# One more seven-product pair in the second FFN of a two-layer decoder trunk: parts of 7, 8 and 7 pairs

## The chip, the cores and the metric

The kernel runs on one core of a Trainium2 chip. The metric is the device time of one execution in microseconds (us). Engines: PE is the matrix engine (TensorE), ACT the scalar engine, DVE the vector engine, POOL is GpSimd, and SP issues most transfers. POOL issues transfers too: those that add into their destination.

## What is computed

Two layers work on 528 positions (16 meta tokens and 512 real ones) of width 1024. Each layer has a mixer and a feed-forward part (FFN), both with a norm before and a norm after:

```python
def ffn_sublayer(h, pre_g, post_g, w_up, conv_w, w_down):
    u = rms_norm(h, pre_g)
    z = jnp.einsum("bld,df->blf", u, w_up)          # 1024 -> 2 x 2816
    z = causal_depthwise_conv(z, conv_w)            # 3 taps
    g, up = jnp.split(z, 2, axis=-1)
    y = jnp.einsum("blf,fd->bld", jax.nn.silu(g) * up, w_down)
    return h + rms_norm(y, post_g)
```

The mixer holds an attention of 8 heads with a forgetting gate, a convolution branch and a short convolution, and ends in a product with `w_out`. Everything is float32.

## The kernel before

**Products.** Each float32 operand is split into a high and a low half (`whi`, `wlo` for a weight, `uhi`, `ulo` for the activations), and each product is three matmuls: high by high, low by high, high by low. Weights arrive in chunks (a `raw` tile of 128x1024), ACT makes the high half and DVE the low half.

**The FFN.** The 2816 hidden channels are 22 pairs `f` (a gate block and an up block of 128 channels each). The pairs are worked in parts, `PARTS = (8, 7, 7)`: after the pairs of a part, the 8 blocks of the down product over that part's pairs run ("downs"), and add into `yp`. The result of pair `f` lies in `y_pair(slot)`, `slot` being its place in its part.

**Ordinary and seven-product pairs.** An ordinary pair is 2 blocks x 8 k-steps x 3 halves x 2 column halves = 96 matmuls (L837). For the pairs listed in `SEVEN` the kernel cuts weights and activations into 2x2 blocks and forms seven block products instead of eight: `seven_pair` runs 7 x 4 k-steps x 3 halves = 84 matmuls of 258 columns in the second layer (L2288). This needs sums of activation blocks (`ts`, made once per layer by the steps of `normalised`, which `build` issues a few at a time), and sums of weight blocks (`w_sum`, four blocks per pair, kept in DRAM).

**Where weight sums are made.** `SUMS[l]` lists the pairs of layer `l` by place: place 0 in the FFN of the layer before, place 1 in the mixer of layer `l`, place 2 in the FFN, places 3 and 4 in the downs of its first two parts. At places 0 to 2 the sums are made by transfers alone (`sum_steps`): three copies issued by SP, then three adding transfers issued by POOL, each reading what the one before it wrote. In the mixer they are offered to the planner at fixed times, one pair every `SUM_EVERY` = 40 us, with `SUM_LAT` = 9 us from one step to the next (L1846 to L1850):

```python
        for i, f in enumerate(sums_at(l, 1)):
            copies, *adds = sum_steps(l, f)
            tok = flow.op("sp", 2.0, copies, (Tok(flow.pe + SUM_EVERY * i),), prio=8, lat=SUM_LAT)
            for op in adds:
                tok = gp(SUM_US, op, tok, prio=8, lat=SUM_LAT)
```

The adding transfers are L534 and the copies L545; a copy is queued on SP behind the last weight load that was issued before it. Where POOL's transfers end up among POOL's other work is decided when the program is built, so it is shown below from the built program.

**The mixer's attention.** For each head and block of keys, PE forms logits (L1637), ACT takes the exponential into `pf` or `p` (L1644), POOL clears the masked triangle with an AFFINE_SELECT (L1651), and PE multiplies `pf` by the values (L1671). Between these PE works on projections and on the first blocks of `w_out` (L837), in one fixed order. Each engine works through its own instructions in order; POOL's transfers wait in the same queue as its AFFINE_SELECTs.

Of the kernel before, what the change touches and what calls it, by code (L numbers as in the profile page):

```python
# [18 lines left out]
KD = D // P  # L19
# [6 lines left out]
CK = 31  # L26
DFF = 2816
NF = DFF // P
PARTS = (8, 7, 7)


SUMS = (((), (11, 12, 13), (15, 16), (17, 18), (19, 20)),
        ((8, 9), (10, 11, 12, 13), (15, 16), (17, 18), (19, 20)))
SEVEN = tuple(sorted(sum(places, ())) for places in SUMS)
NEXT_SUMS, AHEAD_SPLITS = 13, (8, 8, 9, 9, 10, 10, 11)
SUM_US, SUM_LAT, SUM_EVERY = 0.9, 9.0, 40.0
# [46 lines left out]
def chunk_list():  # L83


    out = []
    for l in range(DEPTH):
        def win(*spans, k0=0, kn=KD):
            out.append(("w_in", l, k0, kn, spans))
        for j in range(2):  # L90
            win((C_AG + P * j, P))
            win((C_AV + P * j, P))
        for kind, j in mixer_steps(l):
            if kind == "q":
                win((C_Q + P * j, P))
            elif kind == "k":
                win((C_K + P * j, P))
            elif kind == "v":
                spans = [(C_V + 256 * j, 256)] + ([(C_F, HEADS)] if j == 0 else [])
                win(*spans, k0=0, kn=4)  # L100
                win(*spans, k0=4, kn=4)
            elif kind in SC_COL:
                win((SC_COL[kind] + P * j, P))
            elif kind == "pw":
                out.append(("a_pw_w", l, 0, 2, [(0, 256)]))
        for m in range(KD):
            out.append(("w_out", l, 0, KD, [(P * m, P)]))
        f0 = 0
        for n in PARTS:
            for f in range(f0, f0 + n):  # L110
                out.append(("ffn_w_up", l, 0, KD, [(P * f, P)]))
                out.append(("ffn_w_up", l, 0, KD, [(DFF + P * f, P)]))
            for m in range(KD):
                out.append(("ffn_w_down", l, f0, n, [(P * m, P)]))
            f0 += n
    return out
# [22 lines left out]
def mixer_steps(l):  # L139


    return ORDERS[l]
# [247 lines left out]
def tile_hybrid_trunk(ctx: ExitStack, tc: tile.TileContext, xT, wflat, pv_d, out):  # L390
# [225 lines left out]
    def prep_one():  # L616
        i = wpos[0]
        if i >= len(chunks):
            return
        if i in seven_up:  # L620
            if not parts:
                t = sums[seven_up[i]]
                parts.extend((("c", t[:, 1::2]), ("b", t[:, 0:3:2]), ("d", flat_w(i)[:, SB:])))
            kind, src = parts.popleft()
            wpos[0] += not parts
            raw = raw_tile()
            sz = SB if kind == "d" else 2 * SB
            with ExitStack() as order:
                for x in last if kind == "b" else ():
                    order.enter_context(tc.issue_after(x.ins))  # L630
                load = nc.sync.dma_start(raw[:, :sz] if kind == "d" else raw[:, :sz].rearrange("p (e s) -> p e s", e=2), src)
            if kind == "b":
                hi, lo = (T(tx[0], [P, 2 * SB], F32R, t) for t in ("shi", "slo"))
            elif kind == "c":
                hi, lo = (T(wp, [P, CHUNK], F32R, t) for t in ("whi", "wlo"))
            else:
                hi, lo = y_pair(max(PARTS) - 1)
            with ExitStack() as order:
                for x in last if kind == "b" else ():
                    order.enter_context(tc.issue_after(x.ins))  # L640
                high = nc.scalar.copy(hi[:, :sz], raw[:, :sz])
                last_low[0] = nc.vector.tensor_sub(lo[:, :sz], raw[:, :sz], hi[:, :sz].bitcast(F32))
            last[:] = load, high, last_low[0]
            ready.append((i, tuple(t[:, :sz].rearrange("p (k n) -> p k n", n=P) for t in (hi, lo))))
            return
        wpos[0] += 1
        kn, n = chunks[i][3], chunk_cols(chunks[i])
        sz = kn * n
        raw = raw_tile()
        last_load[0] = nc.sync.dma_start(raw[:, :sz], wflat[offs[i]:offs[i] + P * sz].rearrange("(p s) -> p s", p=P))  # L650
        hi, lo = wtile(i, "whi"), wtile(i, "wlo")
        nc.scalar.copy(hi[:, :sz], raw[:, :sz])  # L652
        last_low[0] = nc.vector.tensor_sub(lo[:, :sz], raw[:, :sz], hi[:, :sz].bitcast(F32))  # L653
        ready.append((i, tuple(t[:, :sz].rearrange("p (k n) -> p k n", n=n) for t in (hi, lo))))
# [1365 lines left out]
    def y_pair(i):  # L2020
        t = T(ypool, [P, 2, L], F32R, f"y{i}")
        return t[:, 0], t[:, 1]
# [6 lines left out]
    with tc.tile_pool(name="pre", bufs=2, reuse_waits="tile") as sp, tc.manual_schedule(engines=every):  # L2029
# [13 lines left out]
        for k in range(KD):  # L2043
            hk, hi, lo, gc = h[:, k, :H], u_raw[0][k], u_raw[1][k], g0[:, k:k + 1]
# [49 lines left out]
    for l in range(DEPTH):  # L2094
# [23 lines left out]
        with tc.tile_pool(name=f"fp{l}", bufs=2, reuse_waits="tile") as fp:  # L2118
# [57 lines left out]
            def ffn_gate(f):  # L2176

                cs = []
                for e, t in enumerate((f, NF + f)):
                    c = T(fp, [P, 2, H], F32, "c", 4).rearrange("p a b -> p (a b)")[:, :2 * fw]  # L2180
                    gate_conv(t, zs[(2 * f + e) % len(zs)], c)
                    cs.append(c)
                nc.scalar.activation(cs[0], cs[0], AF.Silu)
                mul_ins[0] = nc.vector.tensor_mul(cs[0], cs[0], cs[1])
                slot = next(f - sum(PARTS[:p]) for p in range(len(PARTS)) if f < sum(PARTS[:p + 1]))
                ghi, glo = (t[:, :2 * fw] for t in y_pair(slot))
                ghi_ins[f] = nc.scalar.copy(ghi, cs[0])  # L2187
                if f == NF - 1:
                    with tc.issue_after(ghi_ins[f].ins):
                        nc.scalar.preload_act_table_set(EXPSET)  # L2190
                glo_ins[0] = nc.vector.tensor_sub(glo, cs[0], ghi.bitcast(F32))
                return ghi, glo
# [17 lines left out]
            def normalised():  # L2210
# [39 lines left out]
                        yield lambda b=b, k=k: un(b, k)  # L2250
                for k in range(0, K2, 2):
                    if k:
                        yield None
                        yield lambda: block(0)
                        yield None
                    yield lambda: total(2, k, lambda: at(b12), lambda: at(b22))
# [11 lines left out]

            mul_ins, glo_ins, ghi_ins = [None], [None], {}
            ts, n_seven, primed = [], [0], set()  # L2270
            building = [None]

            def build(n):

# [64 lines left out]
            def finish_pair():  # L2339
                if late_ups:  # L2340
                    late_ups.popleft()()

            g = {}
            f0 = 0
            for part, nf in enumerate(PARTS):
                for f in range(f0, f0 + nf):
                    if g:
                        tick(g[max(g)][0][:, :1])
# [25 lines left out]
                            continue  # L2374
                        scaled(i, [ps[:, :, :H]] if i0 == 0 else [ps[:, hf, :iws[hf]] for hf in range(2)])
                    g[f] = ffn_gate(f)
                    if building[0] is not None and f < PARTS[0] - 1:
                        with tc.issue_after(mul_ins[0].ins):
                            build(5)
                finish_pair()  # L2380
                ks = list(range(nf))
                grhs = lambda b, k, hf, f0=f0: g[f0 + k][b][:, fw * hf:fw * (hf + 1)]
                if seven and part == 0:
                    for k in range(0, KD, 4):
                        nc.sync.dma_start(h_dram[:, k:k + 4], h[:, k:k + 4])
                    spare[0] = h
                if part < len(PARTS) - 1:
                    more = down_sums(l, part)
                    for op in more.pop(-1):
                        op()  # L2390
# [100 lines left out]
```

## Time and profile before

| | |
|---|---|
| median of the runs | 1264.51 us (1263.05 to 2452.8, three runs) |
| the profiled execution | 1262.1 us, of which the span from first to last instruction is 1260.4 us |
| PE busy | 1244.2 us (99%) |
| DVE, ACT, POOL busy | 926.0, 710.3, 175.9 us |
| second mixer, second FFN (by the trace) | about 658 to 905 us, then to about 1206 us |

A timeline row gives the start, the duration, the engine, the line, the operation with what it writes and reads, the number of instructions merged, and in brackets the idle time of the engine just before and what ended it. A matmul's duration is longer than its share of the stream, since matmuls overlap: a window's length over its count tells what one costs.

### The profile page before, as it was taken

The numbers are of one execution on the slowest core, as the hardware profiler recorded it, in microseconds if no ns is written. First come the engines' busy times: TensorE is split into PE (matmuls) and PEld (weight loads), VectorE is DVE, ScalarE is ACT, GpSimd is POOL, SyncE is SP. The second block draws the span as 40 slices with busy tenths as digits, with TensorE's granted clock in tenths as the row PEclk, the third lists the DMA queues.
The fourth block names the chain that finished last, engine by engine and source line by source line (L and its number), as shares of the span: only waits on it lengthen the run. The fifth ranks groups of instructions, "written<-read, shape, count | busy, mean of one in ns | idle before, by whom it ended". The sixth has DMA issues, their size and how long they took to land.

```text
span 1260.4 us, 24292 instructions
## 1 busy us (share of the span) xinstructions
PE 1244.2 (99%) x9554; PEld 1194.4 (95%) x9554; DVE 926.0 (73%) x1581; ACT 710.3 (56%) x1377; POOL 175.9 (14%) x360
## 2 busy tenths in 40 slices
PE   8999999999999999999999999999999999999997
PEld 8999898999999999999999988999999899989997
DVE  7887866589874776487688877756799748757954
ACT  7254576655444663476673545775554447526763
POOL 1323411001111001010003244110022000000000
PEclk9999999999999999999999999999999999999999
DMA  7267551726658755765652684547166565465611
GB/s 245 80 154 180 122 118 47 256 88 150 185 146 339 243 192 153 243 193 169 209 186 68 157 194 109 144 116 238 70 166 177 148 212 172 151 228 178 203 60 67
DMA packets 80755, 206.59 MB, mean 164 GB/s; under 512 B 8624, under 2 KB 18992, under 8 KB 80128
## 3 DMA queue, kind: packets, MB, share of 16 engines
q1 hardware_dynamic: 66976, 168.20, 42.1%
q0 software_dynamic: 13664, 36.84, 13.0%
q8 instruction: 75, 1.23, 0.4%
q14 instruction: 40, 0.33, 0.1%
HBM read 170.82 MB, written 50.60 MB: 176 GB/s over the span
## 4 chain that ended last, share of the span: by engine, by line
PE 94%; DVE 2%; ACT 1%; DMA 1%; POOL 1%; issue 0%; SPq 0%; DVEq 0%; ACTq 0%
PE psum L837 63%; PE psum L2288 17%; PE psum L1407 5%; PE psum L1671 3%; PE psum L1637 2%; PE psum L974 1%; PE psum L1593 1%; PE psum L1737 1%; PE psum L1323 1%; DMA raw<-in_w_dram 0%; POOL dm L1608 0%; DMA h<-in_x_dram 0%; DVE yp L1050 0%; DVE h L1060 0%; PE psum L1617 0%
## 5 line engine op out<-in xcount | busy, mean ns | idle before, releaser
L837 PE MATMUL psum<-y,whi 128*128 128x264 f32 (+3 forms) x1968 | 383.8, 299 | 0.8 <-DVE zs L989 0.7
L837 PEld LDWEIGHTS psum<-y,whi 128*128 128x128 f32 x1968 | 305.8, 188 | 13.7 <-DVE zs L989 0.9
L837 PE MATMUL psum<-uhi,whi 128*128 128x264 f32 (+1 forms) x1168 | 292.2, 289 | 1.5 <-ACT uhi L2069 0.8
L837 PE MATMUL psum<-ulo,whi 128*128 128x264 f32 (+1 forms) x1168 | 286.0, 284 | 0.6 <-DVE ulo L2071 0.4
L837 PE MATMUL psum<-uhi,wlo 128*128 128x264 f32 (+1 forms) x1168 | 285.3, 284 | 0.0
L837 PE MATMUL psum<-y,wlo 128*128 128x264 f32 (+3 forms) x984 | 274.0, 297 | 0.7 <-DVE wlo L793 0.7
L837 PEld LDWEIGHTS psum<-uhi,whi 128*128 128x128 f32 x1168 | 201.7, 189 | 5.9 <-issue 1.6
L837 PEld LDWEIGHTS psum<-ulo,whi 128*128 128x128 f32 x1168 | 201.8, 189 | 1.3 <-DVE ulo L2071 0.6
L837 PEld LDWEIGHTS psum<-uhi,wlo 128*128 128x128 f32 x1168 | 201.5, 189 | 0.0
L837 PEld LDWEIGHTS psum<-y,wlo 128*128 128x128 f32 x984 | 178.0, 188 | 6.4 <-DVE wlo L793 1.1
L2173 DVE SCALAR_TENSOR_TENSOR c<-zs,pv,c 128x528 f32<-128x528 f32 (+1 forms) x176 | 130.5, 756 | 21.2 <-ACT c L2171 19.9
L652 ACT CAST whi<-raw 128x1024 fp32r<-128x1024 f32 (+1 forms) x65 | 66.1, 1021 | 96.9 <-PE psum L837 74.3
L793 DVE TENSOR_TENSOR wlo<-raw,whi 128x1024 fp32r<-128x1024 f32 (+2 forms) x80 | 95.6, 1204 | 31.1 <-ACT whi L789 30.5
L789 ACT CAST whi<-raw 128x1024 fp32r<-128x1024 f32 (+2 forms) x80 | 81.7, 1030 | 26.3 <-PE psum L837 18.1
L653 DVE TENSOR_TENSOR wlo<-raw,whi 128x1024 fp32r<-128x1024 f32 (+1 forms) x65 | 76.9, 1183 | 20.9 <-ACT whi L652 20.9
L1153 DVE SCALAR_TENSOR_TENSOR cacc<-apad,pv,cacc 128x528 f32<-128x528 f32 x120 | 87.5, 771 | 0.1
L2288 PE MATMUL psum<-uhi,whi 128*128 128x258 f32 (+1 forms) x252 | 71.4, 284 | 0.0
L2288 PE MATMUL psum<-ulo,whi 128*128 128x258 f32 (+1 forms) x252 | 71.3, 283 | 0.0
L2288 PE MATMUL psum<-uhi,wlo 128*128 128x258 f32 (+1 forms) x252 | 70.8, 283 | 0.0
L2171 ACT ACTIVATE c<-zs,pv 128x528 f32<-128x528 f32 (+1 forms) x88 | 63.0, 727 | 6.8 <-DVE zs L2136 2.6
L2206 POOL COPY cols<-y 128x1 f32<-128x1 f32 x24 | 18.4, 767 | 334.7 <-ACT y L2187 334.4
L2288 PE MATMUL psum<-t,shi 128*128 128x258 f32 (+1 forms) x336 | 63.2, 283 | 0.0
(273 smaller groups left out, 2324.4 us busy)
## 6 DMA issues: line engine op xcount, KB each, us to landing
raw<-in_w_dram SPq DMA_DIRECT2D x114, 512.0 KB, 4.6
raw<-in_w_dram SPq DMA_DIRECT2D x30, 448.0 KB, 5.2
h<-in_w_dram SPq DMA_DIRECT2D x25, 512.0 KB, 4.7
raw<-w_sum SPq DMA_DIRECT2D x21, 512.0 KB, 5.2
h<-w_sum SPq DMA_DIRECT2D x21, 512.0 KB, 5.1
h<-in_w_dram POOLq DMA_DIRECT2D x16, 512.0 KB, 4.0
w_sum<-h POOLq DMA_DIRECT2D x16, 512.0 KB, 6.3
w_sum<-in_w_dram SPq DMA_DIRECT2D x26, 256.0 KB, 5.8
```

The lines of the kernel that those rows point to most:

```text
L652: nc.scalar.copy(hi[:, :sz], raw[:, :sz])
L653: last_low[0] = nc.vector.tensor_sub(lo[:, :sz], raw[:, :sz], hi[:, :sz].bitcast(F32))
L789: nc.scalar.copy(box["hi"][:, :sz], box["raw"][:, :sz])
L793: nc.vector.tensor_sub(lo[:, :sz], box["raw"][:, :sz], box["hi"][:, :sz].bitcast(F32))
L837: nc.tensor.matmul(d, lhsT=w[a][:, k, cols], rhs=rhs(b, k, hf), start=start and i == 0 and p == 0, stop=stop and i == n - 1 and p == 2)
L1153: nc.vector.scalar_tensor_tensor(conv[j], in0=src, in1=conv[j], scalar=col("a_dw_w", CK * j + i), op0=ALU.mult, op1=ALU.add)
L1407: nc.tensor.matmul(ps[:n, :nw], lhsT=(uhi, ulo)[ui][:, k, P * b:P * b + n], rhs=w[wi][:, k % 4, :], start=k == 0 and p == 0, stop=k == KD ...
L1637: nc.tensor.matmul(s, lhsT=k[:, ka:ka + kn], rhs=q[:, s0:qz], start=i == 0, stop=i == 1)
L1671: nc.tensor.matmul(acc[:, s0 - qa:qz - qa], lhsT=vals[:, b].rearrange("p h d -> p (h d)")[:, o:o + P], rhs=box["p"], start=b == 0, stop=b ...
L2171: nc.scalar.activation(dst, src[:, 2:2 + 2 * fw], AF.Copy, scale=wtap(2, t))
L2173: nc.vector.scalar_tensor_tensor(dst, in0=src[:, i:i + 2 * fw], scalar=wtap(i, t), in1=dst, op0=ALU.mult, op1=ALU.add)
L2288: nc.tensor.matmul(psum[:, bank, :n7], lhsT=w[a][:, k0 + k, :], rhs=rhs(b, k), start=start and k == 0 and p == 0, stop=stop and k == K2 - ...
```

## The change

In the second layer the parts become 7, 8 and 7 pairs, and pair 7, so far the last ordinary pair of the first part, becomes the first seven-product pair of the second part: 13 such pairs instead of 12. The weight sums at place 0 are those of pairs 7 and 8 (they were 8 and 9), and the second mixer makes five pairs' sums, 9 to 13 (they were four, 10 to 13). With one pair less before the downs of the first part, `build` issues 20 of the activation-sum steps in the pairs (they were 24) and four more go behind the first downs, together with the next.

```diff
-PARTS = (8, 7, 7)
+PARTS = ((8, 7, 7), (7, 8, 7))
 SUMS = (((), (11, 12, 13), (15, 16), (17, 18), (19, 20)),
-        ((8, 9), (10, 11, 12, 13), (15, 16), (17, 18), (19, 20)))
+        ((7, 8), (9, 10, 11, 12, 13), (15, 16), (17, 18), (19, 20)))
...
-                hi, lo = y_pair(max(PARTS) - 1)
+                hi, lo = y_pair(KD - 1)
...
                 for k in range(0, K2, 2):
                     if k:
-                        yield None
+                        if not downs:
+                            yield None
                         yield lambda: block(0)
                         yield None
...
-                    if building[0] is not None and f < PARTS[0] - 1:
+                    if building[0] is not None and f < PARTS[l][0] - 1:
                         with tc.issue_after(mul_ins[0].ins):
                             build(5)
                 finish_pair()
+                downs.append(part)
```

The other lines of the change read the parts of the layer (`PARTS[l]`) where they read `PARTS`. Slot 7 of `y_pair` holds the last quarter of a seven-product pair's weights; with eight pairs in the second part it also holds that part's last result.

On POOL, in the second mixer, at the attention of the last head, stood before (`w_sum_13` are the sums of pair 13, `pf_10045` and the following are the exponentials of head 7, `p_755` the last of head 6):

```order
L534 DMA w_sum_13_782_8129<-in_w_dram 128x2x512
L1651 AFFINE_SELECT pf_9935<-pf_9935 128x128
L1651 AFFINE_SELECT pf_9949<-pf_9949 128x128
L1651 AFFINE_SELECT pf_9964<-pf_9964 128x128
L1651 AFFINE_SELECT p_755_8078<-p_755_8078 16x16
L1651 AFFINE_SELECT pf_10045<-pf_10045 128x128
L534 DMA w_sum_13_782_8129<-w_sum_13_782_8129 128x512
L1651 AFFINE_SELECT pf_10085<-pf_10085 128x128
```

and with the change (the fourth pair of the mixer is now 12, the fifth 13; `pf_10046` and `pf_10086` are the tiles that were `pf_10045` and `pf_10085`):

```order
L534 DMA w_sum_12_782_8129<-in_w_dram 128x2x512
L1651 AFFINE_SELECT pf_9936<-pf_9936 128x128
L1651 AFFINE_SELECT pf_9950<-pf_9950 128x128
L1651 AFFINE_SELECT pf_9965<-pf_9965 128x128
L1651 AFFINE_SELECT p_755_8078<-p_755_8078 16x16
L534 DMA w_sum_13_783_8130<-in_w_dram 128x2x512
L534 DMA w_sum_13_783_8130<-w_sum_13_783_8130 128x512
L1651 AFFINE_SELECT pf_10046<-pf_10046 128x128
L534 DMA w_sum_12_782_8129<-w_sum_12_782_8129 128x512
L534 DMA w_sum_13_783_8130<-w_sum_13_783_8130 128x512
L1651 AFFINE_SELECT pf_10086<-pf_10086 128x128
```

The three adding transfers of the fifth pair now stand among the last head's AFFINE_SELECTs: two ahead of the first of them, directly behind one another, and the third ahead of the second.

On SP, at the same place, with the change (`raw` tiles are weight chunks of `w_out`, `h` is the residual stream read back):

```order
L545 DMA w_sum_12_782_8129<-in_w_dram 128x512 x2
L545 DMA w_sum_12_782_8129<-in_w_dram 128x1024
L785 DMA raw_9957<-in_w_dram 128x1024
L545 DMA w_sum_13_783_8130<-in_w_dram 128x512 x2
L545 DMA w_sum_13_783_8130<-in_w_dram 128x1024
L785 DMA raw_10271<-in_w_dram 128x1024
```

The three copies of the fifth pair stand behind the load of `raw_9957`; before, the load that is now `raw_10271` followed it at once, and nothing else moved there.

More of the change, by code (lines that the diff above doesn't have):

```diff
@@ L108, in chunk_list @@
         f0 = 0
-        for n in PARTS:
+        for n in PARTS[l]:
             for f in range(f0, f0 + n):
@@ L2184, in ffn_gate @@
                 mul_ins[0] = nc.vector.tensor_mul(cs[0], cs[0], cs[1])
-                slot = next(f - sum(PARTS[:p]) for p in range(len(PARTS)) if f < sum(PARTS[:p + 1]))
+                slot = next(f - sum(PARTS[l][:p]) for p in range(len(PARTS[l])) if f < sum(PARTS[l][:p + 1]))
                 ghi, glo = (t[:, :2 * fw] for t in y_pair(slot))
@@ L2270, in tile_hybrid_trunk @@
             ts, n_seven, primed = [], [0], set()
-            building = [None]
+            building, downs = [None], []
             def build(n):
@@ L2344, in tile_hybrid_trunk @@
             f0 = 0
-            for part, nf in enumerate(PARTS):
+            for part, nf in enumerate(PARTS[l]):
                 for f in range(f0, f0 + nf):
@@ L2386, in tile_hybrid_trunk @@
                     spare[0] = h
-                if part < len(PARTS) - 1:
+                if part < len(PARTS[l]) - 1:
                     more = down_sums(l, part)
```

## The prediction

> **What bounds the kernel now.** First the page's busy times and its chain of what ended last, then PE's waits, over the whole span and in the second FFN:
>
> ```profile
> PE 1244.2 (99%) x9554; PEld 1194.4 (95%) x9554; DVE 926.0 (73%) x1581; ACT 710.3 (56%) x1377; POOL 175.9 (14%) x360
> PE 94%; DVE 2%; ACT 1%; DMA 1%; POOL 1%; issue 0%; SPq 0%; DVEq 0%; ACTq 0%
> PE psum L1617 <- POOL dm L1608: 1.4, 2, 1.0
> PE psum L1671 <- POOL pf L1651: 0.6, 2, 0.3
> ...
> PE psum L837 <- ACT uhi L1066: 0.5, 1, 0.5
> PE psum L837 <- DVE ulo L1068: 0.3, 1, 0.3
> ```
>
> PE carries 94% of the chain and its longest waits anywhere are about a microsecond. The last two rows are all that PE waits for from 895 to 1225 us, and both fall before the pairs of the second FFN. So a matmul taken away there shortens the end by its own length, and a wait put anywhere ahead of PE lengthens the end by its own length: there is no slack on PE to swallow it. POOL is busy 14% of the time, which says little: it matters only where PE waits for it.
>
> **What the change removes.** An ordinary pair has 96 matmuls, a seven-product pair 84. What one costs is a window's length over its count, in the ordinary pairs (925 to 965), the downs (978 to 1023 and 1095 to 1134) and the seven-product pairs (1026 to 1072); the columns are window, length, busy time with count for PE, its weight loads, DVE, ACT, POOL, then granted clock, DMA share and GB/s:
>
> ```profile
> 925.00:965.00 40.00, 40.00 (x337) 40.00 (x336) 37.78 (x67) 18.09 (x25) 9.90 (x13) 1.00 0.73 200
> 978.00:1023.00 45.00, 45.00 (x197) 36.36 (x196) 28.30 (x35) 19.38 (x27) 3.58 (x6) 1.00 0.62 187
> 1026.00:1072.00 46.00, 46.00 (x386) 46.00 (x384) 34.80 (x45) 32.47 (x58) 0.53 (x1) 1.00 0.55 169
> 1095.00:1134.00 39.00, 39.00 (x170) 31.50 (x169) 22.89 (x31) 11.77 (x16) 2.14 (x4) 1.00 0.58 193
> ```
>
> 40.00 / 337 = 0.1187 us and 46.00 / 386 = 0.1192 us. The pair goes from 96 x 0.1187 = 11.40 to 84 x 0.1192 = 10.01: **1.4 us less**. The downs keep their number, 22 pairs x 8 blocks, and only move from the first part to the second. A few records may be missing from a count, but from both alike.
>
> **What hides the rest in the FFN.** The thirteenth pair loads 1.75 MB instead of 1 MB and splits them; in the seven-product window DVE has 11 of 46 us free, ACT 13, and DMA is at 0.55, so I take nothing. The four activation-sum steps that move behind the first downs are three splits and one sum, seven instructions of DVE and ACT, 4.8 us at the 0.69 that a row below has for this size; DVE has 16.7 us free in the first part's downs. If that cover failed, PE would wait 4.8 us at most. The cover of the last pair's result gets thinner: the downs start with two blocks over all pairs but the last.
>
> ```profile
> 977.90 0.64 PE L837 MATMUL psum<-y,whi 128*128 128x512 f32 x2
> 984.06 0.69 DVE L2191 TENSOR_TENSOR y<-c,y 128x512 fp32r<-128x512 f32 x1 [0.69 <-ACT y L2187]
> ```
>
> The downs begin at 977.90 and the last result is there at 984.75, 6.85 us later. A down matmul costs 39.00 / 170 = 0.23, so the cover shrinks from 42 to 36 matmuls, 9.7 to 8.3 us, and still exceeds 6.85 by 1.4. In the second part it grows by as much. Slot 7 makes the load of pair 15's last quarter wait for the second part's last down, but only the seventh product needs it, 6 x 12 matmuls or 8.6 us later; the first part had the same wait before, and PE shows none there. Nothing again.
>
> **What the change adds in the mixer.** Here PE, ACT and DVE keep their order; only POOL and SP change, at the last head. These are POOL's rows there, and those of two places where it already issued a first and a second adding transfer close together:
>
> ```profile
> 687.17 1.18 POOL L534 DMA_DIRECT2D w_sum<-in_w_dram  x1 [0.37 <-issue]
> 694.22 0.85 POOL L534 DMA_DIRECT2D w_sum<-w_sum  x1 [5.87 <-DMA w_sum<-in_w_dram]
> ...
> 824.22 0.38 POOL L1651 TENSOR_SCALAR_AFFINE_SELECT p<-p 16x16 f32<-16x16 f32 x1 [0.35 <-ACT p L1644]
> 830.23 1.28 POOL L1651 TENSOR_SCALAR_AFFINE_SELECT pf<-pf 128x128 f32<-128x128 f32 x1 [5.64 <-ACT pf L1644]
> 831.47 0.84 POOL L534 DMA_DIRECT2D w_sum<-w_sum  x1
> 833.25 0.28 POOL L1651 TENSOR_SCALAR_AFFINE_SELECT pf<-pf 128x128 f32<-128x128 f32 x1 [0.94 <-ACT pf L1644]
> ...
> 926.27 1.20 POOL L534 DMA_DIRECT2D w_sum<-in_w_dram  x1
> 935.89 0.86 POOL L534 DMA_DIRECT2D w_sum<-w_sum  x1 [2.02 <-DMA w_sum<-in_w_dram]
> ```
>
> The second add reads what the first wrote, so POOL itself stands still until that has landed: 694.22 - 687.17 = 7.05 us from issue to issue. At 687 this cost nothing, the attention having not begun. Now the same two stand directly behind one another ahead of the first AFFINE_SELECT of head 7, which ran at 830.23, and the third ahead of the second, which ran at 833.25. When they can start is set by the copies on SP, and how long each takes by the landing times (kilobytes, then median us from issue to landing; the last row is for all of them):
>
> ```profile
> 807.19 1.80 SPq L545 DMA_DIRECT2D w_sum<-in_w_dram  x3
> 821.74 0.33 SPq L785 DMA_DIRECT2D raw<-in_w_dram  x1
> ...
> w_sum<-in_w_dram SPq DMA_DIRECT2D x10, 256.0 KB, 4.8
> w_sum<-in_w_dram SPq DMA_DIRECT2D x5, 512.0 KB, 6.1
> w_sum<-in_w_dram POOLq DMA_DIRECT2D x4, 512.0 KB, 7.0
> w_sum<-w_sum POOLq DMA_DIRECT2D x8, 256.0 KB, 5.0
> ...
> DMA to landing us min/median/max: 4.6/5.6/8.5
> ```
>
> Step by step, in the times of the profile before. The load of the chunk leaves SP at 821.74 + 0.33; the three copies follow, 0.6 us each by the 1.80 of the row above. The second starts at 822.7 and lands 4.8 later, at 827.5; the third starts at 823.3 and lands at 829.4. POOL is free from 824.60 and waits for 827.5: first add. It lands at 834.5: second add, until 835.4. AFFINE_SELECT, 0.3 us: 835.7. Fourth pair's second add, 0.84: 836.5. The fifth pair's third add needs the second landed, 834.5 + 5.0 = 839.5, and is through at 840.3. The second AFFINE_SELECT ends at 840.6. PE asks for them here:
>
> ```profile
> 831.64 0.42 PE L1671 MATMUL psum<-pf,vals 128*128 128x128 f32 x2
> 835.13 0.83 PE L1671 MATMUL psum<-pf,vals 128*128 128x400 f32 x2
> ```
>
> The first is ready at about 835.8 instead of 831.64: PE stands 4.2 us. It then needs 3.5 us to the second, at 839.3, which is ready at 840.7: another 1.4. Queued behind on PE are the first products of `w_out`, then everything else. **Together 5.6 us more.** Bounds: if the first add lands in 9.6 us, as between the rows at 926 and 935 (an upper bound from issue to issue), the sum is 8.2; if the copies too take 8.5 us, the longest landing among these transfers, it is 12. Below, a gain has no reason, since nothing is taken off POOL; nothing lost would need both adds to land before POOL is asked. I take the 7.0 and 5.0 that belong to this very stage.
>
> **The sum.** 1262.1 (the profiled execution; 1.7 us lie around its span) - 1.4 + 5.6 = 1266.3. The two agreeing runs, 1263.05 and 1264.51, lie 1.0 and 2.4 us above that execution, so I add the mean of these, 1.7: **1268**. Against a bound of 2%, about 25 us and what a measurement of this kernel can tell from no change, that is no change.
>
> **The rivals.** First, the wait is hidden: POOL's adds land before PE asks, and only the 1.4 us remain, 1262.1 - 1.4 + 1.7 = 1262.4. For it speaks the plan, whose `SUM_LAT` of 9 us between adds was not meant to let POOL stand; against it the row at 694.22, where POOL stands for the landing. Even with the shortest landing, 4.6 us, for both adds, the two AFFINE_SELECTs end at 833.2 and 837.8, PE loses 1.6 + 1.2 = 2.8 us and the time is 1265. I give 1262 to 1265 together 0.15. A page speaks for this rival: the Trainium skill, "DMA: Bandwidth & Descriptors", section "Anatomy of one DMA — SWDGE (gpsimd) path", fits one of POOL's transfers as 2.0 us plus its bytes at 436 GB/s, an estimate of 3.2 us for 512 KB and 2.6 for 256 KB, with which PE would lose under 1 us here; the landings of 7.0 and 5.0 in the trace differ from it, and the measurement decides.
>
> Second, PE loses its clock in the wait. In the profile PE is never without work this long except at the end:
>
> ```profile
> 1253.25 2.00 PE L1081 MATMUL psum<-yp,ident 128*128 128x256 f32 x8 [1.38 <-DVE yp L1050]
> 1257.00:1260.40 3.40, 0.00 (x0) 0.00 (x0) 0.00 (x0) 0.00 (x0) 0.00 (x0) 0.81 0.60 205
> ```
>
> PE's last work ends at 1255.25, and the granted clock averages 0.81 over the last 3.4 us. If it fell to half, it did so for 1.3 of them, from 1259.1 on, 3.9 us after PE's last work. A wait of 4.2 us is just longer. If the clock is halved for what follows, the 3.5 us of work up to the second wait take up to 7, of which 1.4 was waiting anyway, and some 2 us more go at half rate behind it: 2 to 4 us on top, 1270 to 1272. The Trainium skill, "TensorE: Matmul & The Clock Gate", section "Part 1: The HAM clock gate", has the clock drop to half after an idle window of about 3.4 us, windows running freely; the last row agrees that it drops, and no trace so far shows it in mid-run. I give it 0.25.
>
> Third, on the slower side: the landings are late because the copies, the adds and the weight loads of `w_out` meet. POOL's queue holds PE in any case, so each microsecond past 7.0 or 5.0 goes straight to the end. The price is in the first of these rows:
>
> ```profile
> 455.35 0.53 POOL L589 DMA_DIRECT2D h<-in_w_dram  x1 [31.31 <-DMA w_sum<-in_w_dram]
> ...
> 780.00:840.00 60.00, 59.55 (x430) 54.26 (x430) 41.35 (x99) 43.88 (x116) 15.06 (x33) 1.00 0.53 127
> ```
>
> where POOL stood 31.31 us for a transfer. One such wait instead of 7 gives 1268 + 24 = 1292, over 2% slower. It decides from 25 + 1.4 - 5.6 = some 21 us beyond my landings. Against it: a DMA share of 0.53 in the 60 us around, and the landings of 4.6 to 8.5 us. 0.02 past 2%, and 0.06 for the bounds' upper end, 1271 to 1274.
>
> **How the numbers follow.** My forecast with its own range 1266 to 1270: 0.5. Clock lost: 0.25. Hidden: 0.15. Late landings: 0.08. A cover in the FFN that fails, up to 4.8 us more: 0.02. The range is 1261.5 to 1274, from the hidden case to the upper bound of 12 us. Faster by over 2% is in no case (0.01 is left for the unknown), slower by over 2% 0.02.
>
> **What the profile after would show.** POOL's waits of w_sum on w_sum and on its copies between 824 and 841 us, two of them, of 6 and 3 us or so, and PE's L1671 waiting for POOL pf by 4 and 1 to 2 us; the granted clock in that window; the second FFN 1.4 us shorter from first matmul to last, with no PE wait in it, and 84 more L2288 matmuls. I am wrong if POOL's order on the chip lets AFFINE_SELECTs go ahead, if L1671 shows no wait, or if PE waits at the edge of the first and second part.

## The result, and the profile after

The changed kernel takes 1277.5 us (median of four runs, 1276.7 to 1281.3); the kernel before, run beside it, 1263.1 (of its four runs one was disturbed, 2452.8 us, and is left out here and of the ratio). The ratio is 1.0117, with an interval of 1.0090 to 1.0143: some 14 us slower, within the 2% that I called no change, but 3.5 us above the top of my range.

First the page of the changed kernel (busy times, then the chain of what ended last by engine), and PE's two longest waits:

```profile
PE 1248.4 (98%) x9542; PEld 1198.0 (94%) x9542; DVE 927.9 (73%) x1581; ACT 713.7 (56%) x1385; POOL 175.9 (14%) x363
PE 89%; DVE 4%; DMA 3%; ACT 2%; issue 1%; POOL 1%; SPq 0%; DVEq 0%; ACTq 0%; POOLq 0%
...
PE psum L1671 <- POOL pf L1651: 6.8, 3, 6.3
PE psum L2289 <- ACT whi L652: 4.0, 1, 4.0
```

12 matmuls are gone, as they should be, and yet PE's busy time rose by 4.2 us: some of it ran slowly. PE's share of the chain fell from 94% to 89%, and there are two waits that the kernel before did not have: one for POOL in the mixer, which I had forecast, and one for ACT in the second FFN, which I had not.

To see what each cost, I cut the span at two rows that every version has: the last head's first small product by the values (PE), and the first results of the second FFN (DVE). Of before, then of after:

```profile
828.90 0.34 PE L1671 MATMUL psum<-p,vals 128*128 128x16 f32 x2
900.29 1.38 DVE L2145 TENSOR_TENSOR zs<-psum,rz 128x250 f32<-128x250 f32 x4
...
828.66 0.34 PE L1671 MATMUL psum<-p,vals 128*128 128x16 f32 x2
909.15 1.39 DVE L2145 TENSOR_TENSOR zs<-psum,rz 128x250 f32<-128x250 f32 x4
```

The stretch between the rows, B, went from 71.4 to 80.5 us, 9.1 more. The rest to the end of the span, C, went from 1260.4 - 900.3 = 360.1 to 1275.0 - 909.15 = 365.9, 5.8 more. Ahead of them, A, nothing changed.

**Stretch B.** SP, POOL and PE at the last head of the changed kernel (timeline rows), then windows over the same time:

```profile
821.86 1.85 SPq L545 DMA_DIRECT2D w_sum<-in_w_dram  x3
829.24 1.15 POOL L534 DMA_DIRECT2D w_sum<-in_w_dram  x1 [4.91 <-DMA w_sum<-in_w_dram]
836.61 0.85 POOL L534 DMA_DIRECT2D w_sum<-w_sum  x1 [6.21 <-DMA w_sum<-in_w_dram]
837.18 0.59 POOL L1651 TENSOR_SCALAR_AFFINE_SELECT pf<-pf 128x128 f32<-128x128 f32 x1
842.16 0.83 POOL L534 DMA_DIRECT2D w_sum<-w_sum  x1 [3.51 <-DMA w_sum<-w_sum]
842.71 0.59 POOL L1651 TENSOR_SCALAR_AFFINE_SELECT pf<-pf 128x128 f32<-128x128 f32 x1
837.82 0.80 PE L1671 MATMUL psum<-pf,vals 128*128 128x128 f32 x2 [6.25 <-POOL pf L1651]
844.00 0.83 PE L1671 MATMUL psum<-pf,vals 128*128 128x400 f32 x2
...
836.00:840.00 4.00, 2.18 (x9) 2.18 (x10) 0.00 (x0) 1.22 (x4) 2.00 (x3) 0.57 0.56 84
840.00:844.00 4.00, 4.00 (x15) 3.07 (x15) 0.00 (x0) 0.98 (x4) 1.13 (x2) 0.58 0.61 85
```

POOL stands three times, for the copies and twice for its own adds, and each AFFINE_SELECT comes when the add ahead of it is through. From the small product at 828.66 to the first product that needs `pf` it takes 9.16 us (2.74 before), and from there to the second 6.18 (3.49 before): 6.4 + 2.7 = 9.1. The granted clock is the last figure but two: 0.57 and 0.58 over 8 us mean half rate for (0.43 + 0.42) x 4 / 0.5 = 6.8 us.

**Stretch C.** The chain at the edge of the first part, in order of time (start, length, what), then DVE's row for the low half in it, with the idle time ahead of it, and the windows behind:

```profile
998.87 7.91 DMA raw<-in_w_dram
...
1006.79 0.63 ACT y L641
...
1007.45 0.69 DVE y L642
1008.14 0.61 DVE h L596
...
1009.04 7.66 DMA w_sum<-h
...
1016.72 3.62 DMA h<-in_w_dram
...
1020.44 1.05 ACT whi L652
...
1021.53 0.58 PE psum L2289
...
1007.45 0.69 DVE L642 TENSOR_TENSOR y<-raw,y 128x512 fp32r<-128x512 f32 x1 [2.91 <-ACT y L641]
...
1018.00:1021.50 3.50, 0.00 (x0) 0.00 (x0) 0.00 (x0) 1.06 (x2) 0.00 (x0) 0.91 0.77 254
1021.50:1024.00 2.50, 2.47 (x11) 2.47 (x12) 1.23 (x1) 0.56 (x2) 0.00 (x0) 0.50 0.74 268
1024.00:1027.00 3.00, 3.00 (x16) 3.00 (x15) 0.00 (x0) 0.37 (x1) 0.00 (x0) 0.50 0.20 70
1027.00:1030.00 3.00, 3.00 (x25) 3.00 (x24) 1.56 (x2) 2.32 (x3) 0.00 (x0) 0.88 0.00 0
```

Read from its end: PE waits for the high half of pair 8's gate weights; these were loaded late, into a piece of `h`, the tile whose DRAM copy frees it for weights (`spare_tile`); that piece was still held by pair 18's weight sum, made in the downs (`down_sum`: load, four adds L593 to L596, and a store that POOL issues, though it adds nothing) and stored at 1009.04; the store waited for the last add; and that add stood on DVE behind L642, the low half of pair 7's last quarter, whose load took 7.9 us: DVE was idle for 2.91 us ahead of it. PE's order, fixed when the program is built, asks for pair 8's weights behind only 24 of pair 7's 84 matmuls. PE stands 4.0 us and then runs at half rate for about 6.8 again (0.6 + 2.5 + 3.0 + 0.7).

### The profile page after: what moved, and what is told of

It reads as the page before. It is cut to its first block, busy times and chain, and to the rows that moved or that the text cites. A ratio compares the mean times of both kernels' runs of the same rounds, so it can differ in the third digit from the quotient of the medians.

```text
span 1275.0 us, 24298 instructions
## 1 busy us (share of the span) xinstructions
PE 1248.4 (98%) x9542; PEld 1198.0 (94%) x9542; DVE 927.9 (73%) x1581; ACT 713.7 (56%) x1385; POOL 175.9 (14%) x363
## 4 chain that ended last, share of the span: by engine, by line
PE 89%; DVE 4%; DMA 3%; ACT 2%; issue 1%; POOL 1%; SPq 0%; DVEq 0%; ACTq 0%; POOLq 0%
PE psum L837 58%; PE psum L2289 17%; PE psum L1407 4%; PE psum L1671 3%; PE psum L1637 2%; PE psum L974 1%; DMA raw<-in_w_dram 1%; DMA w_sum<-in_w_dram 1%; PE psum L1593 1%; PE psum L1323 1%; PE psum L1737 1%; DMA w_sum<-h 1%; POOL dm L1608 0%; DVE wlo L793 0%; DVE yp L1050 0%
## 5 line engine op out<-in xcount | busy, mean ns | idle before, releaser
L837 PE MATMUL psum<-uhi,whi 128*128 128x264 f32 (+1 forms) x1136 | 284.9, 289 | 1.5 <-ACT uhi L2069 0.7
L837 PE MATMUL psum<-ulo,whi 128*128 128x264 f32 (+1 forms) x1136 | 279.1, 284 | 0.6 <-DVE ulo L2071 0.4
L837 PE MATMUL psum<-uhi,wlo 128*128 128x264 f32 (+1 forms) x1136 | 278.8, 283 | 0.0
L837 PEld LDWEIGHTS psum<-uhi,whi 128*128 128x128 f32 x1136 | 196.4, 188 | 5.9 <-issue 1.6
L837 PEld LDWEIGHTS psum<-ulo,whi 128*128 128x128 f32 x1136 | 196.6, 188 | 1.3 <-DVE ulo L2071 0.6
L837 PEld LDWEIGHTS psum<-uhi,wlo 128*128 128x128 f32 x1136 | 196.4, 188 | 0.0
L652 ACT CAST whi<-raw 128x1024 fp32r<-128x1024 f32 (+1 forms) x64 | 65.0, 1018 | 88.8 <-PE psum L837 71.7
L2289 PE MATMUL psum<-uhi,whi 128*128 128x258 f32 (+1 forms) x264 | 75.7, 287 | 4.0 <-ACT whi L652 4.0
L2289 PE MATMUL psum<-ulo,whi 128*128 128x258 f32 (+1 forms) x264 | 75.3, 286 | 0.0
L2289 PE MATMUL psum<-uhi,wlo 128*128 128x258 f32 (+1 forms) x264 | 74.5, 285 | 0.0
L2289 PE MATMUL psum<-t,shi 128*128 128x258 f32 (+1 forms) x352 | 67.3, 286 | 0.0
```

The lines of the kernel that those rows point to most:

```text
L837: nc.tensor.matmul(d, lhsT=w[a][:, k, cols], rhs=rhs(b, k, hf), start=start and i == 0 and p == 0, stop=stop and i == n - 1 and p == 2)
L2289: nc.tensor.matmul(psum[:, bank, :n7], lhsT=w[a][:, k0 + k, :], rhs=rhs(b, k), start=start and k == 0 and p == 0, stop=stop and k == K2 - ...
```

## The experiments

Each run's stretches, from its own profile (us; A ends at the last head's first small product, B at the first L2145 of the second FFN, which is L2147 where lines were added, C at the end of the span):

| kernel | A | B | C | median | ratio to before, interval |
|---|---|---|---|---|---|
| before | 828.9 | 71.4 | 360.1 | 1262.3 to 1263.8 | 1 |
| changed | 828.7 | 80.5 | 365.9 | 1277.5 | 1.0117 (1.0090 to 1.0143) |
| e1 five sums only | 831.0 | 79.0 | 360.1 | 1272.0 | 1.0070 (1.0055 to 1.0085) |
| e5 parts only | 830.1 | 71.4 | 359.9 | 1263.3 | 0.9998 (0.9989 to 1.0008) |
| e6 sums of the downs early | 830.0 | 80.8 | 363.9 | 1277.5 | 1.0115 (1.0098 to 1.0132) |
| e7 sums moved | 833.6 | 71.4 | 366.1 | 1270.9 | 1.0058 (1.0043 to 1.0073) |
| e8 one add first | 831.3 | 81.1 | 359.2 | 1273.1 | 1.0081 (1.0066 to 1.0096) |
| e9 candidate | 829.2 | 71.4 | 359.0 | 1262.0 | 0.9997 (0.9987 to 1.0008) |
| e10 busy at the edge | 829.1 | 81.3 | 363.8 | 1277.3 | 1.0119 (1.0101 to 1.0136) |
| e11 busy in the mixer | 830.8 | 82.5 | 365.9 | 1278.4 | 1.0124 (1.0105 to 1.0143) |
| e12 less busy | 828.3 | 80.0 | 361.2 | 1277.1 | 1.0114 (1.0090 to 1.0138) |
| e13 five, spread | 829.0 | 71.7 | 359.9 | 1263.9 | 1.0012 (1.0003 to 1.0021) |
| e14 candidate again | 828.0 | 71.4 | 359.3 | 1262.6 | 1.0001 (0.9992 to 1.0010) |

Each ratio is to the kernel before as it ran in the same session: its median there was 1263.1 beside the changed kernel, 1263.8 beside e1 and e5 to e7, 1263.1 beside e8 to e11, 1262.3 beside e12 to e14.

A is nearly the same program in all of them and still differs by up to 5.6 us, so a single time tells little here and the stretches tell more. (Part of e7's long A is a wait of 1.84 us in the first layer, with half rate behind it; see the last section.) Where PE doesn't wait, B is 71.4 in five kernels, and C is 359.9 to 360.1 in the three with twelve seven-product pairs and 359.0 to 359.9 in the four with thirteen (e8, e9, e13, e14).

**e1, one part alone: five pairs' sums in the mixer.**

```diff
-        ((8, 9), (10, 11, 12, 13), (15, 16), (17, 18), (19, 20)))
+        ((8,), (9, 10, 11, 12, 13), (15, 16), (17, 18), (19, 20)))
```

> The kernel before, with its parts of 8, 7 and 7 pairs and its twelve seven-product pairs, but with pair 9's sums made in the second mixer (five pairs there, 9 to 13) and only pair 8's at place 0. Theory (the change loses time at two places that have nothing to do with each other, the last head of the mixer and the edge of the first part): L1671 waits 6 us for POOL and the clock halves there, as in the changed kernel, so 1263.8 + 8.9 = 1272.7, and nothing in the second FFN. Rival (the wait at the part's edge follows from the late mixer, which shifts loads against work): that wait shows here too, and the time is 1277 or more. Second rival (the mixer's loss comes from the whole set of the changed kernel's loads, not from the fifth pair's sums): 1264.

Measured 1272.0 against 1263.8. B is 7.6 us longer and C unchanged; PE waits 5.8 us at L1671 and nowhere in the second FFN. The two losses are separate, and the mixer's belongs to the fifth pair's sums.

**e5, the other part alone: the parts of 7, 8 and 7 with pair 7 ordinary** (twelve seven-product pairs; the sums of before).

```diff
-        ((7, 8), (9, 10, 11, 12, 13), (15, 16), (17, 18), (19, 20)))
+        ((8, 9), (10, 11, 12, 13), (15, 16), (17, 18), (19, 20)))
```

> The changed kernel's parts of 7, 8 and 7 pairs, but with pair 7 an ordinary pair, now the first of the second part: the twelve seven-product pairs and the weight sums of the kernel before. Here the last add of pair 18's sum stands ahead of the low half of the first seven-product pair's last quarter on DVE, as it did before; in the changed kernel it stands behind it. Theory a (it is DVE's order: the add waits for a quarter that was loaded late): no wait at the edge, 1264. Theory b (the first part's downs, 7/8 as long, no longer cover store and load through the spare tile): the edge waits 2.6 to 4.0 us and the clock halves behind it, 1267 to 1271. In both, nothing is lost in the mixer.

Measured 1263.3; no wait, C 359.9. With the pairs in this order shorter downs cost nothing. It doesn't prove DVE's order, though, nor clear the shorter downs: here PE has a whole ordinary pair to do between the downs and the first seven-product pair. e8 is the cleaner test.

**e6, the downs' second sum wholly earlier** (in the second layer; j is the sum's number in its part, the numbers are the blocks of the downs behind which load, add and store are issued).

```diff
-            for m, op in ((2 * j - 1, load), (2 * j + 1, add), (2 * j + 1 + (j < 2), store)):
+            for m, op in zip(((-1, 1, 2), (-1, 2, 3), (3, 5, 5))[j] if l else (2 * j - 1, 2 * j + 1, 2 * j + 1 + (j < 2)), (load, add, store)):
```

> The changed kernel, with the sums in the downs of the second layer made earlier: the loads of the second pair of sums are issued ahead of the downs together with the first pair's, its adds behind block 2 instead of 3 and its store behind block 3 instead of 4. Theory (the edge of the first part waits for the spare tile, which that store holds; the clock halves because PE waits 4 us): wait and half clock both go, 1277.5 - 4.0 - 3.4 = 1270 (the mixer's 8.9 stays, less 1.4 for the lighter pair 7). Rival (the half clock there has another cause than this wait): only the 4.0 go, 1273.5. Rival (another chain is close behind the removed one): 1274 to 1277.

Measured 1277.5: nothing gained in the median, 2.0 us in C. The wait only moved. With the sums over earlier, the kernel hands out the spare tiles earlier as well, and now a weight chunk of the last down block is loaded, at 1009.09, into a piece that the store of pair 17's sum held until then. PE's longest wait from 905 to 1225 us, and windows:

```profile
PE psum L837 <- ACT whi L652: 2.7, 1, 2.7
...
1016.00:1018.00 2.00, 2.00 (x6) 1.56 (x6) 2.00 (x4) 1.84 (x3) 0.00 (x0) 0.51 0.63 169
1018.00:1019.00 1.00, 1.00 (x3) 0.75 (x3) 1.00 (x1) 0.00 (x0) 0.00 (x0) 0.50 1.07 369
1019.00:1019.50 0.50, 0.50 (x3) 0.36 (x2) 0.13 (x1) 0.00 (x0) 0.00 (x0) 0.55 0.80 299
```

A wait of 2.7 us was enough to bring half rate, for 3.4 us this time (2.0 + 1.0 + 0.45). This is the rival "another chain is close behind".

**e7, e6 with other places for the sums**, so that the mixer makes four.

```diff
-        ((7, 8), (9, 10, 11, 12, 13), (15, 16), (17, 18), (19, 20)))
+        ((7, 8), (9, 10, 11, 12), (15, 16), (13, 17), (18, 19, 20)))
```

> As the run with the earlier sums, and the second mixer makes four pairs' sums again (9 to 12): those of 13 and 17 are made in the downs of the first part, those of 18, 19 and 20 in the downs of the second. Theory (nothing but the two places lost time, so without both the lighter pair 7 is worth what its matmuls are): 1263.8 - 1.4 = 1262.4, between 1261 and 1264. Rival (three pairs' sums are too many for the second part's downs, and its edge waits as the first one's did): 4 us of wait and 3.4 of clock, 1270.

Measured 1270.9, the rival's figure. B is back at 71.4. C is 366.1: PE waits 3.1 us where e6 waited, with half rate behind it, and 1.5 us at the second part's edge, where three sums are one too many; behind the 1.5 the clock stays at 1.00.

**e8, the second pair's adds one block earlier.**

```diff
-            for m, op in ((2 * j - 1, load), (2 * j + 1, add), (2 * j + 1 + (j < 2), store)):
+            for m, op in ((2 * j - 1, load), (2 * j + 1 - (l and part == 0 and j), add), (2 * j + 1 + (j < 2), store)):
```

On DVE this turned, among others (first the changed kernel, then e8; `y_1155` takes the low half of pair 7's last quarter)

```
L642 TENSOR_TENSOR y_1155_11949<-raw_11947,y_1155_11949 128x512
L596 TENSOR_TENSOR h_10242<-h_10242 128x512
```

into

```
L596 TENSOR_TENSOR h_10242<-h_10242 128x512
...
L642 TENSOR_TENSOR y_1155_11949<-raw_11947,y_1155_11949 128x512
```

> The changed kernel, with one thing moved: in the first part's downs of the second layer the adds of the second pair of sums come behind block 2 instead of block 3, and so ahead of the low half of pair 7's last quarter on DVE instead of behind it; their loads and their store stay where they were in the program, and the downs are as short as in the changed kernel. Theory a (DVE's order made the wait): the last add ends some 5 us earlier, the store lands and the spare tile is loaded before PE asks, and the edge of the first part has no wait and no half clock; the second FFN gets 311.2 - 304.3 = 6.9 us shorter, 1277.5 - 6.9 = 1270.6. Theory b (the shorter downs made it): 2.6 us of wait stay and the clock halves behind them, 1276.

Measured 1273.1. C is 359.2, within 0.2 of theory a's 365.9 - 6.9 = 359.0. The median is 2.5 us above theory a's; in the profiled run A and B are 2.7 and 0.6 longer than the changed kernel's. The rows of e8: DVE's last add and the low half, POOL's store, and the load into the spare tile with ACT's high half, then the two waits that remain in the whole second FFN:

```profile
1004.39 0.67 DVE L596 TENSOR_TENSOR h<-h 128x512 f32<-128x512 f32 x1
1012.39 0.69 DVE L642 TENSOR_TENSOR y<-raw,y 128x512 fp32r<-128x512 f32 x1 [3.97 <-ACT y L641]
...
1005.36 0.53 POOL L601 DMA_DIRECT2D w_sum<-h  x1 [1.82 <-DVE h L596]
1013.50 0.42 SPq L650 DMA_DIRECT2D h<-in_w_dram  x1
1019.23 1.05 ACT L652 CAST whi<-h 128x1024 fp32r<-128x1024 f32 x1 [0.21 <-DMA h<-in_w_dram]
...
PE psum L837 <- ACT uhi L1066: 0.5, 1, 0.5
PE psum L837 <- DVE ulo L1068: 0.2, 1, 0.2
```

The low half is as late as ever, but the add no longer stands behind it, the store is out 7 us ahead of it, and PE finds its weights, though not by much: their high half is through at 1020.28, and PE's first matmul with it starts at 1020.93. The downs are as short as in the changed kernel, so with these downs it is the place of the adds that makes the wait. The edit moved all four adds of pair 18, not only the last, and with them the planner moved three loads on SP and a few of PE's matmuls; that the one low half made most of the delay is read from the 2.91 us that DVE idled ahead of it in the changed kernel, not shown by this run.

**e9 and e14, both repairs: a candidate.** On top of e8, pair 13's sums in the first downs and pair 17's by transfers in the second FFN, so that the mixer makes four and no downs make three.

```diff
-        ((7, 8), (9, 10, 11, 12, 13), (15, 16), (17, 18), (19, 20)))
+        ((7, 8), (9, 10, 11, 12), (15, 16, 17), (13, 18), (19, 20)))
```

> As the run before, and the second mixer makes four pairs' sums again (9 to 12), pair 17's are made by transfers in the second FFN (place 2), and those of 13 and 18 in the downs of the first part, of 19 and 20 in those of the second: no part's downs make three. Theory (the two places were all that the change lost, the lighter pair 7 is worth its twelve matmuls): 1263.8 - 1.4 = 1262.4. Rival (pair 17's transfers or three times two sums hold the spare tiles or SP's queue somewhere else): 1264 to 1270, with a wait at another edge.

> The candidate of run e9 again, with more rounds. Theory: the second FFN and the end took 359.0 us there against 360.1 before, so 1.1 us less than the kernel before, a ratio of 0.9991. Rival: no difference, 1.000.

Measured 1262.0 against 1263.1 in the one session and 1262.6 against 1262.3 in the other: the loss is gone, and nothing can be told from the kernel before. In the profiles C is 359.0 and 359.3, so 0.8 to 1.1 us of the 1.4 are there; the intervals of the two ratios reach 1.1 to 1.3 us to either side, too wide to tell such a gain from none. The candidate is no improvement that I can claim.

**e10, more work at the edge.**

```diff
-                    nc.tensor.matmul(by, lhsT=ones_r, rhs=uhi[:, 0, h7[0][0]:h7[0][1]], start=True, stop=True)
+                    for _ in range(34 if l and n else 1):
+                        nc.tensor.matmul(by, lhsT=ones_r, rhs=uhi[:, 0, h7[0][0]:h7[0][1]], start=True, stop=True)
```

> The changed kernel, with 33 more matmuls of 258 columns (33 x 0.119 = 3.9 us; their result is overwritten) at the edge of the first part, about as long as PE waited there. Their order also lets pair 7's further products go ahead of pair 8's first. Theory (the wait's second half is the clock: PE stands 4 us, then runs at half rate for 6.8 us, which costs 3.4): PE does not stand, the clock stays, and the time falls by what half rate cost though PE has 3.9 us more work: 1277.5 - 3.4 = 1274.1. Rival (half rate costs nothing there, since other engines set the pace in those microseconds): 1277.5.

The median, 1277.3, says the rival, but its four runs go from 1275.9 to 1280.3 and its B is longer than the changed kernel's. In C, 363.8, the theory holds in kind: with 3.9 us more work on PE and a new wait of 0.7 it is 2.1 us shorter, and the clock stays at 1.00. 359.1 (e8 and e9) + 3.9 + 0.7 = 363.7 accounts for it. The changed kernel's 365.9 is 359.1 + 4.0 of wait + 2.8, and these 2.8 are the half rate; I had expected 3.4, but by the windows 0.6 of its 6.8 us fell into the wait itself. The planner split the 34 matmuls, though:

```profile
1018.51 2.31 PE L2313 MATMUL psum<-uhi,ones_r 128*128 128x258 f32 x18
1027.39 2.07 PE L2313 MATMUL psum<-uhi,ones_r 128*128 128x258 f32 x16
```

18 stand where PE waited, the other 16 behind most of pair 7's products and ahead of pair 8's first, for whose weights PE now asks at 1029.30. So the wait shrank to 0.7 by PE's new order too, not by the filling alone; that order without the filling, a third possible repair, was not run.

**e11 and e12, more work in the mixer's wait.**

```diff
             o = 2 * pr * VW + 2 * e
+            for _ in range(100 if l and hd == HEADS - 1 and qa == b == 0 else 0):
+                nc.tensor.matmul(acc[:, :P], lhsT=ones_r, rhs=ones_r, start=True, stop=True)
```

(58 for 100 in e12.)

> The changed kernel, with 100 more matmuls of 128 columns (some 6 us; their result is overwritten) ahead of the last head's first product by the values, where PE waited 6.25 us. Theory a (POOL sets the end there: the second AFFINE_SELECT is through at 843.3 and the product that needs it started at 844.0): the clock is worth 0.6 to 0.7 us, 1276.8, and PE now waits some 2 us at the second of these products. Theory b (half rate costs 3.4 us here as at the edge): 1274.

> The changed kernel with 58 more matmuls of 128 columns, not 100, ahead of the last head's first product by the values: one took 0.105 us in the run with 100 (38 in a window of 4.00 us), so 100 were 10.5 us and longer than the wait that they were to fill; 58 are 6.1. Theory a (POOL's second wait sets the end of the place and half rate is hidden in it): PE stands some 2 us at the second product that needs POOL, and from the last head's first small product (p by vals) to the start of the second FFN's first results it takes 71.4 + 6.4 + 2.0 = 79.8 us, 0.7 less than the changed kernel's 80.5. Theory b (half rate costs 3.4 us): 77 us there, and 1274.

e11 was mis-sized: a matmul of 128 columns took 0.105 us, not the 0.06 I had assumed, so PE worked through both waits and longer, and B of 82.5 decides nothing. e12 fits theory a: B 80.0 against the 79.8 that it gave. Its PE and POOL rows (L1673 is the L1671 of the other kernels), and the window in which the filled wait ends:

```profile
837.46 0.43 PE L1673 MATMUL psum<-pf,vals 128*128 128x128 f32 x2
842.99 0.94 PE L1673 MATMUL psum<-pf,vals 128*128 128x400 f32 x2 [1.86 <-POOL pf L1651]
841.80 0.83 POOL L534 DMA_DIRECT2D w_sum<-w_sum  x1 [3.65 <-DMA w_sum<-w_sum]
...
836.00:840.00 4.00, 4.00 (x31) 3.71 (x31) 0.00 (x0) 1.66 (x5) 2.00 (x3) 1.00 0.59 87
```

With the clock at 1.00 throughout, PE only waits 1.9 us at the second product instead of crawling up to it. Half rate cost about 0.5 us in the mixer. (The median of e12 is no help: its runs go from 1271.2, the profiled one, to 1280.8. In the profiled one PE waits 1.6 us at the FFN's edge, and the clock doesn't fall there.)

**e13, five pairs in the mixer at other times**, with e8's add.

```diff
-SUM_US, SUM_LAT, SUM_EVERY = 0.9, 9.0, 40.0
+SUM_US, SUM_LAT, SUM_EVERY = 0.9, 9.0, 34.0
```

> Five pairs' sums in the second mixer as in the changed kernel, but offered to the planner every 34 us instead of every 40, with the earlier add at the edge of the first part as in the run e8. Pair 12's first two adding transfers now stand directly behind one another where POOL has nothing else for 17.6 us (788.65 to 806.68 in the changed kernel's trace); pair 13's first stands alone ahead of the last head's AFFINE_SELECTs, its copies issued one head earlier, its second and third behind all of the AFFINE_SELECTs but the last. Theory (not the number of pairs but the place of two adds that depend on one another, ahead of work that PE needs, made the loss): no wait at L1671, 1263.1 - 1.4 = 1261.7, and 71.4 us from the last head's first small product to the second FFN. Rival (five pairs' transfers are too many for the mixer, wherever they stand): a wait of 4 to 6 us at dm (L1608) or at pf (L1651), 1267 to 1272.

Measured 1263.9, B 71.7. POOL's rows for pair 12's first two adds, some 40 us ahead of the last head, and for the last head:

```profile
788.72 1.19 POOL L534 DMA_DIRECT2D w_sum<-in_w_dram  x1 [0.31 <-issue]
797.12 0.86 POOL L534 DMA_DIRECT2D w_sum<-w_sum  x1 [7.21 <-DMA w_sum<-in_w_dram]
...
825.52 1.23 POOL L534 DMA_DIRECT2D w_sum<-in_w_dram  x1 [0.81 <-issue]
830.36 1.28 POOL L1651 TENSOR_SCALAR_AFFINE_SELECT pf<-pf 128x128 f32<-128x128 f32 x1 [3.61 <-ACT pf L1644]
837.17 0.87 POOL L534 DMA_DIRECT2D w_sum<-w_sum  x1 [0.17 <-issue]
842.03 0.82 POOL L534 DMA_DIRECT2D w_sum<-w_sum  x1 [3.95 <-DMA w_sum<-w_sum]
```

POOL still stands 7.2 us between two adds, but at 789, where nobody waits for it; ahead of the last head's AFFINE_SELECTs is one add that depends on none just ahead of it. So five pairs' sums fit, and the loss was the place. The time is 2 us above what I expected (3 against the kernel before of the same session), and 0.03 to 0.21% above the kernel before: the repaired change is no gain either.

## Why the prediction was wrong, step by step

By the spans, 4.2 us more were forecast and 14.6 measured. The 10.4 between them are 6.8 at the FFN's edge, 3.5 in the mixer, 0.4 for the pair, less 0.2 in A (rounded).

- **What hides the rest in the FFN: this step failed.** Its first sentence took nothing for the thirteenth pair's loads and splits, because DVE has 11 of 46 us free in a window. The time was there, but one of these splits, the low half of pair 7's last quarter, stood 2.91 us for its load, and the last add of pair 18's sum stood behind it. The step did not ask who holds the pieces of `h` that take the next pairs' weights, or what stands on DVE ahead of the add that frees one. (Its other answers, on the activation sums, the last pair's result and slot 7, held.) "PE waits at the edge of the first and second part" stood in the prediction only as a sign that would prove me wrong, and a failing cover got 0.02 and at most 4.8 us. It was 4.0 of wait and 2.8 of half rate. The chain stood in the trace of before (DVE's add and low half, then POOL's store and SP's load):

```profile
1009.35 0.68 DVE L596 TENSOR_TENSOR h<-h 128x512 f32<-128x512 f32 x1
1024.98 0.69 DVE L642 TENSOR_TENSOR y<-raw,y 128x512 fp32r<-128x512 f32 x1
...
1010.33 0.53 POOL L601 DMA_DIRECT2D w_sum<-h  x1 [4.69 <-DVE h L596]
1016.98 0.42 SPq L650 DMA_DIRECT2D h<-in_w_dram  x1
```

Pair 18's last add stood 15.6 us ahead of the low half of a last quarter (there pair 8's, the first of the seven-product pairs); behind it came its store and a spare-tile load that SP issued after a wait for that store, with downs to 1022.7 to cover all this. The change took 5.6 us from these downs and put the low half in front of the add. e8 shows that with the downs as short the adds' place decides. The shorter downs had a part too, by a sum that no run tests: PE waited 4.0 us, and with 5.6 us more of downs ahead it would have asked for these weights after they were there.

- **What the change adds in the mixer: right in mechanism and place, too small in size.** POOL's order, its three stands and PE's two waits came as described. The terms: POOL's first add started at 829.24 instead of 827.5, since the copies landed later; it held the next add for 7.4 instead of 7.0, from issue to issue, and that one the third for 5.55 instead of 5.0. Together the second AFFINE_SELECT was through at 843.3, not 840.7: 2.6 us. Half rate added 0.5 to 0.7, and PE came to the head 0.2 us earlier than before. 5.6 became 9.1 (7.6 to 9.9 in e1, e6, e8 and e10), inside the bounds of 12 that I had given and partly the rival of late landings.
- **The rival of the lost clock** came true, twice, but not with its price: in the mixer 2 to 4 us were forecast and 0.5 to 0.7 came, because PE would have waited for POOL anyway in the time that half rate took. At the edge, where nothing else held PE, it was 2.8. Shorter waits than it reckoned with brought half rate too (last section).
- **What the change removes: 1.4 forecast, 0.8 to 1.1 measured** by C in e8, e9 and e14, and 0.3 in e13, which has the thirteen pairs too. From pair 7's first matmul to pair 14's first, e13 takes 60.4 us and the other three 59.6 to 59.8, so it loses there. In e9 the pairs ahead of the first downs take 61.1 us against 72.6 before, those ahead of the second downs 82.4 against 72.1: 11.5 less and 10.3 more, where 11.40 and 10.01 were forecast. Why the added pair costs more than its share of the window is open.
- **Slot 7 and the second part's edge** cost nothing, as said. Landings as long as the 2% would have needed never came near.

## What to carry to other kernels

Where buffers are lent from one user to another, a change of order must be followed through the loan: who frees the buffer, behind what that instruction stands on its engine, and how long the store takes that comes after it. A queue that works in order makes any instruction that waits for a load a wait for all behind it, so one that frees something belongs ahead of one that waits, and two transfers that depend on each other belong where nobody needs their engine. And a wait on PE of 2 to 3 us or more may have half rate behind it and should be priced with it, unless something else holds PE in those microseconds.

## What the runs showed of the hardware

Half rate came in multiples of one length: 3.4 us behind the wait of 2.7 in e6, 6.8 behind those of 4.0 and 6.25 in the changed kernel, 10.2 in the mixers of e6 and e10, behind 6.2 and 7.1. By the windows it began between 2.2 and 5.0 us after PE had fallen idle: 5.0 in the mixer of the changed kernel and 3.3 at its FFN's edge, nearly 5 at the edge of e6, when PE had had work again for 2 us. Often the work behind a wait pays, not the wait. No length of wait divides the cases: none came behind 1.5 (e7), 1.6 and 1.9 (e12), but 3.4 us came in e7's first layer behind 1.84, as this row and window show ((1.00 - 0.66) x 5 / 0.5 = 3.4):

```profile
111.58 0.34 PE L1593 MATMUL psum<-k,q 128*16 128x16 f32 x2 [1.84 <-DMA k<-g_dram]
...
111.00:116.00 5.00, 4.42 (x24) 4.44 (x25) 1.66 (x9) 0.00 (x0) 1.21 (x4) 0.66 0.34 102
```

The Trainium skill, "TensorE: Matmul & The Clock Gate", section "Part 1: The HAM clock gate", has windows of about 3.4 us that run freely, an idle one to halve the clock and a busy one to restore it. The lengths, and that the wait's own length decides so little, agree with it; that 2.7 and 1.84 us of idling sufficed does not, if a window must be idle from end to end.

The adding transfers of 512 KB from DRAM to DRAM held the next one for 7.4 us (829.24 to 836.61) in the changed kernel, for 7.2 to 8.0 in the same place of e1, e6, e8 and e10 to e12, and for 8.4 in another place of e13 (788.72 to 797.12), so a wait for them varies by most of a microsecond from run to run.
